# Pooling mixer's output projection with tokens on the partitions, six of its sixteen units by seven block products

## The chip, the core and the metric

The kernel runs on one core of one Trainium2 chip. The metric is the device time of one execution in microseconds (us); lower is better. A core has five engines that matter here, each with its own instruction queue, worked off strictly in order: TensorE (PE in the profile), VectorE (DVE), ScalarE (ACT), GpSimd (POOL) and SyncE (SP), which here only issues DMAs. Engines wait for one another and for DMAs through semaphores. TensorE writes its sums into PSUM, everything else lies in SBUF, 128 partitions wide.

## What is computed

A two-layer decoder trunk for 256 tokens of 2048 channels, all in float32. Layer 0 mixes tokens by causal pooling, layer 1 by dilated attention; each mixer and each convolutional feed-forward (FFN) is followed by a layer norm of the residual sum. The change touches layer 0's mixer and its norm:

```python
def pool_mixer(h, w_in, w_grp, scale, w_out):
    p = (h @ w_in).reshape(B_, S, N_POOL_GROUPS, POOL_GROUP_DIM)
    ...                                   # trailing mean over 2, 4, 8, 16 tokens, minus the token
    mixed = jnp.einsum('bsgc,gcd->bsgd', pooled, w_grp).reshape(B_, S, D) * scale
    return mixed @ w_out
...
mix = pool_mixer(h, pool_w_in[i], pool_w_grp[i], pool_scale[i], pool_w_out[i])
h = layer_norm(DEEPNORM_ALPHA * h + mix, ln1_g[i], ln1_b[i])
ff = conv_ffn(h, ...)
```

The 2048 channels are handled as four blocks of 512, and `w_out` as sixteen squares of 512 by 512.

## The kernel before

All weight products run as a list of **units** (`units`, line 69). One unit is a 512-by-512 square of a weight matrix (1 MB in float32) times 256 tokens. To keep float32 accuracy every operand is split into a high part, rounded to TensorE's fp32r format, and a low remainder; three of the four products of the parts are summed. For each weight square ScalarE casts the high part (line 99, tile `wh`) and VectorE subtracts it to get the low part (line 100, tile `wl`).

`run_units` (line 141) writes the program out by hand, and each engine works in just this order. For unit i it first calls `ahead(i)`: SyncE gets the load of unit i+5 (three raw buffers, line 41), and ScalarE and VectorE get the split of unit i+3. The pool for split weights has four buffers (line 42), so the split of unit i+3 can start only when TensorE has finished unit i-1, and must be done when unit i+2 ends. Then come TensorE's products of unit i, then callbacks that earlier units deferred with `later(n, fn)` ("n units from now", line 135), then the unit's own `post`.

Two layouts of a product occur:

- **Features on the partitions** (`mm_quad`, line 165): the weight square is the stationary operand, the tokens stream. Mode "ab" issues 16 matmuls of 512 columns (line 180) and 16 of 256 (line 181) for a unit; mode "a" issues 48 of 256 columns (lines 183 to 185). Mode "x" (also lines 183 to 185, 258 columns) serves the first unit group behind a norm, before the norm's mean and scale are known: it streams XP, the shifted residual times the norm's gain, and corrects afterwards (`norm_evac`, line 471).
- **Tokens on the partitions** (`group_tm`, line 202): the activations are stationary, the weights stream; a plain unit is 24 matmuls of 512 columns (lines 255 to 257). Here a unit can also be done by seven block products instead of eight (`mk_seven`, line 219): it stands in the list as two entries, "a" with 18 and "b" with 24 matmuls of 256 columns (lines 244 to 246). The seven products need sums of blocks of the weights: `split_sums` (line 107) has VectorE compute them (lines 120, 122, 124) beside the splits (lines 119 and 121 for "a", 113 and 114, twice each, for "b"). They also need the same sums of the activations. This form serves the FFN's down projections and the attention's V.

**Before the stage in question**, `x_quad` (line 538) transposes the loaded x (tiles `xin`) on TensorE, splits it, and copies it to the residual H, features on the partitions (line 553). Units 0 to 18 are the input projection and three of the four group products; units 19 to 35 are the sixteen output squares with the last group product as unit 21; the FFN begins at unit 36. `grp_post` (line 526) scales a group's result and splits it into the tile `mixed`.

**The stage itself** (`add_last`, line 487) has features on the partitions, twelve units in mode "ab" and the last four, which make the last column block, in mode "a". `resid_last` (line 331) adds each finished column block to H. After block 0 a matmul with ones estimates the mean of each token from these 512 channels (`shift`, line 382), and all of H is shifted by it. For blocks 1 and 2 `stats` (line 377) accumulates sums and squares, folded by VectorE and squared by ScalarE; `xp` (line 419) makes XP with four ScalarE and four VectorE instructions per block. `chain` (line 430), one unit after the last, makes mean and variance by two matmuls with ones and VectorE's reciprocal of 256 columns, and starts the normalisation.

**Transposing a finished block** exists already, between the FFN's parts: `to_tokens` and `to_features` (lines 798 and 828) transpose 32-by-32 blocks on VectorE and move the blocks to their places with sixteen DMAs of 32 KB (`moves`, line 812), all issued by SyncE in three parts of 6, 5 and 5, one, two and three units later. `early_post` (line 840) recombines the seven products; with `by_dma` GpSimd adds the result by an accumulating DMA (line 287).

Of the kernel before, what the change touches and what calls it, by code (L numbers as in the profile page):

```python
# [32 lines left out]
def trunk(ctx: ExitStack, tc: tile.TileContext, x, pool_w_in, pool_w_grp, pool_scale, pool_w_out,  # L33
# [168 lines left out]
    def group_tm(w, r0s, c0, ncol, xqs, post, apart=False, seven=(), early=None):  # L202
# [5 lines left out]
        def opened():  # L208
            t = pair("t")
            ps.append(t[:, 0, :])  # L210
            if not apart:
                ps.append(t[:, 1, :])
            if seven:
                t = pair("s")
                ps.extend([t[:, 0, :], t[:, 1, :]])
# [3 lines left out]
        def mk_seven(kind, j):  # L219
            fst, fin, op, cl = j == 0, j == len(r0s) - 1, j == opening, j == closing  # L220

            def go(h, l):
                if kind == "a" and fst:
                    opened()
                x, sums = xqs[j](), seven[j]()
# [204 lines left out]
    def chain(ps, lay, which, after):  # L430
# [9 lines left out]
        V.tensor_tensor(mr, ps[:, :T], rs, OP.mult)  # L440
        mb, rb = rm[:, 1:2, :].to_broadcast([P, 4, T]), rm[:, 0:1, :].to_broadcast([P, 4, T])
# [50 lines left out]

    PADW = 16
# [32 lines left out]
    def grp_post(g):  # L526
        def post(ps):
            mixed_q[g] = t = quad_tile("mixed")
            for m in range(4):
# [6 lines left out]
    XIN = {}  # L536

    def x_quad(q, halves=(0, 1)):
        xin = XIN
        if halves[0] == 0:  # L540
            H[q] = hp.tile([P, 4, T], F32, name="h", tag="h")
            XC[q] = quad_tile("xc")
        for half in halves:
            ps = bank("xT")
            for kk in range(2):
                for t in range(2):
                    k = 2 * half + kk
                    PE.transpose(ps[:, kk * T + t * P:kk * T + t * P + P], xin[q, t][:, k * P:(k + 1) * P], ident)
# [4 lines left out]
            before.setdefault(q, []).append(lambda s=s, pv2=pv2: A.copy(H[q][:, s, :], pv2))  # L553
# [4 lines left out]
    def add_grp(g):  # L558
# [9 lines left out]
    add_grp(1)  # L568
    mark = len(units)
    add_last(pool_w_out[0], [(512 * j, 512) for j in (3, 2, 1, 0)], [lambda j=j: mixed_q[j] for j in (3, 2, 1, 0)],  # L570
             True, 0, 0, after=lambda q: to_tokens(q))
# [222 lines left out]

    HT = {}


    def to_tokens(q):
        if q == 0:
            ST["hb"] = hp.tile([P, 4, T], F32, name="hb", tag="h")  # L800
        hb = ST["hb"]
        hf = hb.rearrange("p m t -> p (m t)")
        V.transpose(hf.rearrange("p (t m c) -> p m t c", t=2, m=4), H[q].rearrange("p m (t c) -> p m t c", t=2))

        def to():
            HT[q] = hp.tile([P, 4, T], F32, name="ht", tag="h").rearrange("p a t -> p (a t)").rearrange(
                "p (t c) -> p t c", t=2)
            return HT[q].rearrange("p t c -> p (t c)")

        moves(hf, to)  # L810

    def moves(fr, to):
        fr = fr.rearrange("p (k b j) -> p b k j", k=8, b=4)
        dst = []

        def part(i, n):
            if i == 0:
                dst.append(to().rearrange("p (k a j) -> p a k j", k=8, a=4))
            for ab in range(i, i + n):
                a, b = ab // 4, ab % 4  # L820
                nc.sync.dma_start(dst[0][32 * b:32 * b + 32, a], fr[32 * a:32 * a + 32, b])

        for k, (i, n) in enumerate(((0, 6), (6, 5), (11, 5))):
            later(k + 1, lambda i=i, n=n: part(i, n))

    def to_features(c):
        hb = hp.tile([P, 4, T], F32, name="hb", tag="h")
        hf = hb.rearrange("p m t -> p (m t)")  # L830
        V.transpose(hf.rearrange("p (m t c) -> p t m c", m=4, t=2), HT[c].rearrange("p t (m c) -> p t m c", m=4))

        def to():
            H[c] = hp.tile([P, 4, T], F32, name="h", tag="h")
            return H[c].rearrange("p m t -> p (m t)")

        moves(hf, to)


    def early_post(c, by_dma):  # L840
        def post(p16, p75):
            w = w4("w")
# [444 lines left out]
```

## Time and profile before

| | before |
|---|---|
| median of three runs | 2016.0 us (2015.46 to 2016.46) |
| profiled execution, time | 2015.77 us |
| its span in the trace | 2014.0 us |
| granted clock, mean over the core | 1.00 |
| VectorE busy | 1734.3 us |
| ScalarE busy | 1270.8 us |

How to read it: the profile is of one execution; the 1.8 us between its time and its span lie outside the instructions. Busy times on TensorE overlap, since a matmul's modelled duration runs on into the next; the spacing of the starts tells what a matmul costs. In the lists of instruction groups the columns are line, engine, operation, tiles written and read, shapes, count, then busy time in us and the mean duration in ns, then the engine's idle time before them and what ended it. In the timeline they are start in us, duration in us, engine, line, operation, tiles, shapes and count, and in brackets the idle time before and what ended it.

### The profile page before, as it was taken

The page shows a single profiled execution, that of the slowest core. Times are in us where ns is not written, and L with a number is a line of the kernel's source. Part 1 is how long each engine was busy: PE and PEld are TensorE (multiplying, and loading weights), DVE is VectorE, ACT ScalarE, POOL GpSimd, SP SyncE. Part 2 cuts the span into 40 slices and gives each one's busy share as a digit, 9 for nine tenths or more (in the row PEclk, how much of TensorE's full clock was granted, in tenths as well). Part 3 has the DMA queues.
Part 4 walks back from the last instruction along what each step waited for, and adds up shares of the span by engine and source line. Part 5 has one row for each costly group of instructions (what it writes and reads, how often), then busy time and mean ns, then how long its engine had stood idle before and what let it go on. Part 6 is the DMA issues. An engine that isn't in the chain of part 4 may idle for free.

```text
span 2014.0 us, 31469 instructions
## 1 busy us (share of the span) xinstructions
PE 2005.6 (100%) x12760; PEld 1809.8 (90%) x12760; DVE 1734.3 (86%) x1824; ACT 1270.8 (63%) x1552; POOL 93.1 (5%) x153
## 2 busy tenths in 40 slices
PE   9999999999999999999999999999999999999999
PEld 8898988999899988889888988998899989989987
DVE  6868887999899899879896878787899899989898
ACT  6444686767766676656554445487767677667673
POOL 2000000000000000000001021000000000000000
PEclk9999999999999999999999999999999999999999
DMA  8555466566656757885565657557566756666665
GB/s 264 205 205 186 163 210 192 181 221 223 198 198 200 240 179 229 227 233 188 154 220 173 208 173 204 188 188 211 167 221 202 226 184 224 206 211 190 211 211 186
DMA packets 271297, 407.77 MB, mean 202 GB/s; under 512 B 74430, under 2 KB 85588, under 8 KB 270896
## 3 DMA queue, kind: packets, MB, share of 16 engines
q1 hardware_dynamic: 259488, 388.93, 58.1%
q0 software_dynamic: 11232, 16.18, 5.4%
q8 instruction: 100, 1.64, 0.3%
q10 hardware_dynamic: 432, 0.66, 0.1%
q14 instruction: 45, 0.37, 0.1%
HBM read 380.01 MB, written 2.10 MB: 190 GB/s over the span
## 4 chain that ended last, share of the span: by engine, by line
PE 93%; DVE 4%; DMA 1%; ACT 1%; issue 0%; SPq 0%; DVEq 0%; ACTq 0%
PE acc L180 42%; PE acc L181 21%; PE s L246 3%; PE s L244 3%; PE s L245 3%; PE acc L184 2%; PE acc L185 2%; PE acc L183 2%; PE t L246 2%; PE t L244 2%; PE t L245 2%; PE t L255 1%; PE t L256 1%; PE t L257 1%; DVE wl L100 1%; ACT wh L99 1%
## 5 line engine op out<-in xcount | busy, mean ns | idle before, releaser
L180 PE MATMUL acc<-xc,wh 128*128 128x512 f32 x3264 | 1151.4, 396 | 0.0
L181 PE MATMUL acc<-xc,wl 128*128 128x256 f32 x3264 | 915.7, 281 | 0.9 <-DVE wl L100 0.9
L100 DVE TENSOR_TENSOR wl<-raw,wh 128x2048 fp32r<-128x2048 f32 (+2 forms) x304 | 654.7, 2161 | 168.9 <-ACT wh L99 167.5
L180 PEld LDWEIGHTS acc<-xc,wh 128*128 128x128 f32 x3264 | 615.9, 189 | 142.9 <-issue 0.3
L99 ACT CAST wh<-raw 128x2048 fp32r<-128x2048 f32 (+2 forms) x304 | 546.8, 1805 | 166.2 <-PE acc L180 68.3
L181 PEld LDWEIGHTS acc<-xc,wl 128*128 128x128 f32 x3264 | 615.3, 189 | 1.3 <-DVE wl L100 1.2
L113 ACT CAST wh<-raw 128x1024 fp32r<-128x1024 f32 x144 | 150.6, 1053 | 203.5 <-DVE raw L122 184.1
L114 DVE TENSOR_TENSOR wl<-raw,wh 128x1024 fp32r<-128x1024 f32 x144 | 171.8, 1221 | 11.3 <-ACT wh L113 11.3
L121 DVE TENSOR_TENSOR wl<-raw,wh 128x1536 fp32r<-128x1536 f32 x72 | 126.1, 1752 | 6.4 <-ACT wh L119 5.2
L119 ACT CAST wh<-raw 128x1536 fp32r<-128x1536 f32 x72 | 106.4, 1478 | 36.6 <-PE acc L180 28.0
L287 POOL DMA_DIRECT2D ht<-w x48 | 41.3, 1014 | 1446.4 <-DVE ht L873 721.6
L246 PE MATMUL t<-wh,g 128*128 128x256 f32 x376 | 105.7, 281 | 0.0
L244 PE MATMUL t<-wh,g 128*128 128x256 f32 x376 | 105.7, 281 | 0.0
L245 PE MATMUL t<-wl,g 128*128 128x256 f32 x376 | 105.5, 281 | 0.0
L616 ACT ACTIVATE c<-u,cv 128x256 f32<-128x256 f32 x172 | 89.6, 594 | 24.0 <-DVE f L678 17.4
L246 PE MATMUL s<-wh,xs 128*128 128x256 f32 x344 | 95.9, 279 | 0.0
L244 PE MATMUL s<-wh,xs 128*128 128x256 f32 x344 | 95.8, 279 | 0.0
L245 PE MATMUL s<-wl,xs 128*128 128x256 f32 x344 | 95.7, 278 | 0.0
L124 DVE TENSOR_TENSOR raw<-raw 128x1024 f32<-128x1024 f32 x72 | 88.2, 1225 | 2.5
L621 ACT ACTIVATE a<-u,cv 128x256 f32<-128x256 f32 x172 | 73.5, 500 | 11.9 <-DVE g L688 11.9
L607 ACT COPY u<-acc 128x512 f32<-128x512 f32 x84 | 46.9, 573 | 46.3 <-PE acc L181 46.0
L621 ACT ACTIVATE u<-u,cv 128x256 f32<-128x256 f32 x172 | 73.4, 499 | 0.0
(339 smaller groups left out, 3442.3 us busy)
## 6 DMA issues: line engine op xcount, KB each, us to landing
raw<-in_ffn_w_up_dram SPq DMA_DIRECT2D x160, 1024.0 KB, 4.9
raw<-in_ffn_w_down_dram SPq DMA_DIRECT2D x80, 1024.0 KB, 5.1
raw<-in_pool_w_out_dram SPq DMA_DIRECT2D x16, 1024.0 KB, 5.0
raw<-in_shared_w_k_dram SPq DMA_DIRECT2D x16, 1024.0 KB, 5.2
raw<-in_attn_w_q_dram SPq DMA_DIRECT2D x16, 1024.0 KB, 5.1
raw<-in_shared_w_v_dram SPq DMA_DIRECT2D x16, 1024.0 KB, 5.2
raw<-in_attn_w_o_dram SPq DMA_DIRECT2D x16, 1024.0 KB, 5.2
ht<-w POOLq DMA_DIRECT2D x50, 256.0 KB, 5.2
```

The costliest lines, as they stand in the source:

```text
L99: A.copy(wh[i][:, s], r[:, s])
L100: V.tensor_tensor(wl[i][:, s], r[:, s], wh[i][:, s].bitcast(F32), OP.subtract)
L113: A.copy(h[:, :, n], r[:, :, n])
L114: V.tensor_tensor(l[:, :, n], r[:, :, n], h[:, :, n].bitcast(F32), OP.subtract)
L119: A.copy(hs, rs)
L121: V.tensor_tensor(ls, rs, hs.bitcast(F32), OP.subtract)
L180: PE.matmul(ps[m].ap, h[:, k, c], q[:, k, :, :T], start=st, stop=False)
L181: PE.matmul(ps[m][:, :T], l[:, k, c], q[:, k, 0, :T], start=False, stop=sp)
L244: PE.matmul(to, xh, h[:, k, n], start=opens and kk == 0, stop=False)
L245: PE.matmul(to, xh, l[:, k, n], start=False, stop=False)
L246: PE.matmul(to, xl, h[:, k, n], start=False, stop=ends and kk == 1)
L621: A.activation(to[:, m, :], u[:, m, i:i + T], AF.Copy, scale=cv[:, i, j:j + 1])
```

## The change

The output projection of the pooling mixer is done with tokens on the partitions, as four column blocks of four units. The residual is x as loaded: the x tiles are now the tiles `HT` (tokens on the partitions) themselves, and the copies to H are gone. Block 0 has four plain units. Blocks 1 and 2 have the order plain, seven, plain, seven, and block 3 plain, seven, seven, plain; the six units by seven products are those whose activations come from groups 0 and 1. In the list of units the entries then are: block 0 at 19, 20, 22 and 24 (the last group product at 21, block 1's first unit at 23), block 1's rest 25 to 29, block 2 30 to 35, block 3 36 to 41, and the FFN from 42 on.

`summed` replaces `grp_post`'s work for groups 0 and 1 and makes the block sums of the activations. The statistics are VectorE's batch-norm statistics per token (`bn_stats`, one value set per partition); the shift is the mean of block 0 per token, added by ScalarE to all eight half tiles (`begin`). Each finished block goes back to features on the partitions by `to_features`, whose definition, with that of `to_tokens`, `moves` and `early_post`, stands earlier in the file; the last block's sixteen moves go at once over the queues of SyncE (seven), GpSimd (six) and ScalarE (three). XP is made six units after a block's end (two for the last block). `chain_tm` replaces `chain`: it spreads the per-token scale and mean over the partitions by four 128-column transposing matmuls, one unit after the end. The second PSUM buffer of a seven-product group is opened at its first seven-product entry.

The diff, cut to its core:

```diff
+        def opened_seven():
+            t = pair("s")
+            ps.extend([t[:, 0, :], t[:, 1, :]])
...
+    def chain_tm(mvs, lay, which, after):
+        st = w4("st")
+        for t in range(2):
+            for i, col in ((0, 3), (2, 4)):
+                A.activation(st[:, i + t, :P], onesd, AF.Copy, scale=mvs[t][:, col:col + 1])
+        def spread():
+            ps = bank("spread")
+            for i in range(4):
+                PE.matmul(ps[:, P * i:P * i + P], st[:, i, :P], ident, start=True, stop=True)
+            rm = lnp.tile([P, 4, T], F32, name="rm", tag="sq")
+            A.activation(rm[:, 0:2, :].rearrange("p a t -> p (a t)"), ps, AF.Copy, scale=float(D))
+            ...
+            normed(rm, lay, which, after)
+        later(1, spread)
...
+    def moves(fr, to, at_once=False):
...
+            for ab in range(i, i + n):
+                a, b = ab // 4, ab % 4
+                by = (nc.sync, nc.gpsimd, nc.sync, nc.gpsimd, nc.scalar)[ab % 5] if at_once else nc.sync
+                by.dma_start(dst[0][32 * b:32 * b + 32, a], fr[32 * a:32 * a + 32, b])
...
+    def summed(g, ps):
+        x = w4("mix")
+        for m in range(4):
+            A.activation(x[:, m, :], ps[m][:, :T], AF.Copy, scale=vec[0][:, 64 + 4 * g + m:65 + 4 * g + m])
+        split_act(mixed_q[g], x)
...
+        def two():
+            V.tensor_tensor(d[0], a21, a22, OP.add)
+            V.tensor_tensor(d[1], d[0], a11, OP.subtract)
+            V.tensor_tensor(d[2], a21, a11, OP.subtract)
+            V.tensor_tensor(d[3], a12, d[1], OP.subtract)
...
+            A.copy(hl[0], f)
+            V.tensor_tensor(hl[1], f, hl[0].bitcast(F32), OP.subtract)
...
+        later(1, two)
...
-            before.setdefault(q, []).append(lambda s=s, pv2=pv2: A.copy(H[q][:, s, :], pv2))
...
+    def out_post(c):
+        def post(t, ps, half=None):
+            y = HT[c][:, t, :]
+            if c == 0:
+                V.scalar_tensor_tensor(y, y, ALPHA, ps, op0=OP.mult, op1=OP.add)
+            else:
+                V.tensor_tensor(y, y, ps, OP.add)
+            if c == 3:
+                ended(t)
+            elif t == 1:
+                if c == 0:
+                    later(1, begin)
+                later(2, lambda: landed(c))
+                later(6, lambda: xp(c, 0, 0))
+        return post
+
+    def begin():
+        ST["bn"] = bn = lnp.tile([P, 2, 5, 6], F32, name="bn", tag="bn")
+        for t in range(2):
+            mv = lnp.tile([P, 6], F32, name="mv", tag="mv", bufs=2)
+            V.bn_stats(bn[:, t, 0, :], HT[0][:, t, :])
+            V.bn_aggr(mv[:, 0:2], bn[:, t, 0:1])
+            V.tensor_scalar(mv[:, 2:3], mv[:, 0:1], -1.0, None, op0=OP.mult)
+            V.tensor_scalar(bn[:, t, 0, 1::3], bn[:, t, 0, 1::3], mv[:, 0:1], None, op0=OP.subtract)
+            for c in range(4):
+                y = HT[c][:, t, :]
+                A.activation(y, y, AF.Identity, scale=1.0 if c == 0 else ALPHA, bias=mv[:, 2:3])
+
+    def landed(c):
+        if c > 0:
+            for t in range(2):
+                V.bn_stats(ST["bn"][:, t, c, :], HT[c][:, t, :])
+        to_features(c)
+
+    def ended(t):
+        ...
+        V.bn_stats(bn[:, t, 3, :], HT[3][:, t, :])
+        V.bn_aggr(mv[:, 0:2], bn[:, t, :4])
+        A.activation(mv[:, 2:3], mv[:, 1:2], AF.Sqrt, bias=epst)
+        if t == 1:
+            to_features(3, True)
+        V.reciprocal(mv[:, 3:4], mv[:, 2:3])
+        V.tensor_tensor(mv[:, 4:5], mv[:, 0:1], mv[:, 3:4], OP.mult)
+        ends.append(mv)
+        if t == 1:
+            chain_tm(ends, 0, 0, to_tokens)
+            later(2, lambda: xp(3, 0, 0))
+
-    add_last(pool_w_out[0], [(512 * j, 512) for j in (3, 2, 1, 0)], [lambda j=j: mixed_q[j] for j in (3, 2, 1, 0)],
-             True, 0, 0, after=lambda q: to_tokens(q))
+    for c, js in enumerate(((3, 2, 1, 0), (3, 1, 2, 0), (3, 1, 2, 0), (3, 1, 0, 2))):
+        sv = {i: (lambda j=j: msums[j]) for i, j in enumerate(js) if c > 0 and j < 2}
+        group_tm(pool_w_out[0], [(512 * j, 512) for j in js], 512 * c, 512, [lambda j=j: mixed_q[j] for j in js],
+                 out_post(c), seven=sv, early=early_post(c, c < 3))
...
-                XIN[q, t] = stp.tile([P, 512], F32, name=f"xin{q}{t}")
+            HT[q] = ht_tile()
```

More of the change, by code (lines that the diff above doesn't have):

```diff
@@ L224, in go @@
                     opened()
+                if kind == "a" and op:
+                    opened_seven()
                 x, sums = xqs[j](), seven[j]()
@@ L490, in add_last, with to_tokens, to, ht_tile @@
                   mode="a" if c == 3 else "ab")
+    HT = {}
+    def to_tokens(q):
+        if q == 0:
+            ST["hb"] = hp.tile([P, 4, T], F32, name="hb", tag="h")
+        hb = ST["hb"]
+        hf = hb.rearrange("p m t -> p (m t)")
+        V.transpose(hf.rearrange("p (t m c) -> p m t c", t=2, m=4), H[q].rearrange("p m (t c) -> p m t c", t=2))
+        def to():
+            HT[q] = ht_tile()
+            return HT[q].rearrange("p t c -> p (t c)")
+        moves(hf, to)
+    def ht_tile():
+        return hp.tile([P, 4, T], F32, name="ht", tag="h").rearrange("p a t -> p (a t)").rearrange(
+            "p (t c) -> p t c", t=2)
@@ new lines, in to_features, with to, early_post, post @@
+    def to_features(c, at_once=False):
+        hb = hp.tile([P, 4, T], F32, name="hb", tag="h")
+        hf = hb.rearrange("p m t -> p (m t)")
+        V.transpose(hf.rearrange("p (m t c) -> p t m c", m=4, t=2), HT[c].rearrange("p t (m c) -> p t m c", m=4))
+        def to():
+            H[c] = hp.tile([P, 4, T], F32, name="h", tag="h")
+            return H[c].rearrange("p m t -> p (m t)")
+        moves(hf, to, at_once)
+    def early_post(c, by_dma):
+        def post(p16, p75):
+            w = w4("w")
+            right, left, u5, u = (w[:, i, :] for i in range(4))
+            A.copy(left, p16[:, :256])
+            V.tensor_tensor(right, left, p16[:, 256:], OP.add)
+            V.tensor_tensor(u, right, p75[:, :256], OP.add)
+            y0, y1 = HT[c][:, 0, :], HT[c][:, 1, :]
+            w2 = w.rearrange("p a n -> p (a n)")
+            if by_dma:
+                V.tensor_tensor(w[:, 0::2, :], w[:, 0::3, :], p75[:, 256:].unsqueeze(1).to_broadcast([P, 2, 256]), OP.add)
+                ST["onto"] = [(y0, w2[:, :512]), (y1, w2[:, 512:])]
+                return
+            V.tensor_tensor(y0, y0, w2[:, :512], OP.add)
+            y1 = y1.rearrange("p (a n) -> p a n", a=2)
+            V.tensor_tensor(y1, y1, w[:, 3:4, :].to_broadcast([P, 2, 256]), OP.add)
+            yr = HT[c][:, :, :256]
+            V.tensor_tensor(yr, yr, p75[:, 256:].unsqueeze(1).to_broadcast([P, 2, 256]), OP.add)
+        return post
@@ L547, in x_quad @@
                     k = 2 * half + kk
-                    PE.transpose(ps[:, kk * T + t * P:kk * T + t * P + P], xin[q, t][:, k * P:(k + 1) * P], ident)
+                    PE.transpose(ps[:, kk * T + t * P:kk * T + t * P + P], HT[q][:, t, k * P:(k + 1) * P], ident)
             pv2 = ps.rearrange("p (k t) -> p k t", k=2)
@@ L812, in moves @@
[L812 to L824, printed above, removed]
@@ L1153, in trunk @@
         for q in range(NQ):
-            for t in range(2):
-                XIN[q, t] = stp.tile([P, 512], F32, name=f"xin{q}{t}")
+            HT[q] = ht_tile()
             halves = [slice(0, 256), slice(256, 512)] if q == 0 else [slice(0, 512)]
@@ L1185, in trunk @@
         pools["pool"] = pp
-        pools["pb"] = [pp.tile([P, 4, PADW + T], F32, name=f"pb{i}") for i in range(2)]
+        pools["pb"] = [pp.tile([P, 4, PADW + T], F32, name=f"pb{i}", tag="pb", bufs=2) for i in range(2)]
         for b in pools["pb"]:
```

73 lines of the change are left out of this document (27 added, 46 removed).

## The prediction

> **What bounds the kernel now.** I read the page first: span, engine shares, busy tenths, the chain that ended last.
>
> ```profile
> span 2014.0 us, 31469 instructions
> PE 2005.6 (100%) x12760; PEld 1809.8 (90%) x12760; DVE 1734.3 (86%) x1824; ACT 1270.8 (63%) x1552; POOL 93.1 (5%) x153
> ...
> PE 93%; DVE 4%; DMA 1%; ACT 1%; issue 0%; SPq 0%; DVEq 0%; ACTq 0%
> ```
>
> TensorE sets the time, and a shorter product shows in full as long as weights, activations and statistics keep ahead of it. VectorE, at 86%, is the next to watch. So I looked at the output projection's own stretch, 120.4 us (unit 19 starts) to 216.4 us (the FFN starts), and at its later part.
>
> ```profile
> 120.40:216.40 96.00, 96.00 (x627) 87.42 (x626) 70.82 (x74) 44.69 (x48) 0.00 (x0) 1.00 0.55 187
> 154.15:216.40 62.25, 62.25 (x419) 57.26 (x418) 50.44 (x57) 30.27 (x34) 0.00 (x0) 1.00 0.55 187
> 137.35:159.83 22.48, 22.48 (x130) 19.61 (x129) 13.88 (x13) 8.48 (x6) 0.00 (x0) 1.00 0.54 186
> ```
>
> Columns: window, its length, then busy time of PE, weight loads, DVE, ACT, POOL. VectorE works 70.8 of 96 us here, ScalarE 44.7. The third window is four "ab" units: 5.62 us each.
>
> **TensorE's part of the change.** Prices are distances between starts.
>
> ```profile
> 480.25 0.28 PE L244 MATMUL s<-wh,xs 128*128 128x256 f32 x1
> ...
> 480.84 0.28 PE L246 MATMUL s<-wh,xs 128*128 128x256 f32 x1
> 805.91 0.40 PE L255 MATMUL t<-wh,g 128*128 128x512 f32 x1
> ...
> 806.61 0.40 PE L255 MATMUL t<-wh,g 128*128 128x512 f32 x1
> 222.23 0.60 PE L431 MATMUL acc<-S,onesd 128*128 128x256 f32 x2
> 222.91 0.47 PE L183 MATMUL acc<-xp,wh 128*128 128x258 f32 x1
> 11.98 0.98 PE L548 MATMUL xT<-ident,xin 128*128 128x128 f32 x7 [0.36 <-DMA xin<-in_x_dram]
> ```
>
> Five 256-column steps take 0.59 us: 0.118 each. Three 512-column steps take 0.70: 0.233 each. A plain token-major unit is 24 x 0.233 = 5.60 us, one by seven products 42 x 0.118 = 4.96 us (entry a 2.1, b 2.8), a mode "a" unit 48 x 0.118 = 5.66. Before: 12 x 5.62 + 4 x 5.66 = 90.1 us. After: 10 x 5.60 + 6 x 4.96 = 85.8. The shift's matmul goes (0.12), and the chain's two (222.23 to 222.91: 0.68) become four of 128 columns, about 0.11 apart, seven lasting 0.98 in the row: 0.44. TensorE saves 4.3 + 0.1 + 0.2 = **4.7 us**, if nothing makes it wait.
>
> **VectorE's part.** The price of a seven-product unit's weights:
>
> ```profile
> L100 DVE TENSOR_TENSOR wl<-raw,wh 128x2048 fp32r<-128x2048 f32 x264 | 602.7, 2288 | 155.1 <-ACT wh L99 154.0
> 478.67 0.68 DVE L120 TENSOR_TENSOR raw<-raw 128x512 f32<-128x512 f32 x1
> 479.27 1.75 DVE L121 TENSOR_TENSOR wl<-raw,wh 128x1536 fp32r<-128x1536 f32 x1
> 481.06 0.69 DVE L122 TENSOR_TENSOR raw<-raw 128x512 f32<-128x512 f32 x1
> 481.78 1.22 DVE L124 TENSOR_TENSOR raw<-raw 128x1024 f32<-128x1024 f32 x1
> 482.93 2.42 DVE L114 TENSOR_TENSOR wl<-raw,wh 128x1024 fp32r<-128x1024 f32 x2
> L425 DVE SCALAR_TENSOR_TENSOR xp<-h,vec,xp 128x256 fp32r<-128x256 f32 x48 | 20.0, 479 | 0.0
> L831 DVE STREAM_TRANSPOSE hb<-ht 128x1024 f32<-128x1024 f32 x4 | 5.0, 1239 | 0.1
> L882 DVE BATCH_NORM_STATS2 bn<-ht 128x6 f32<-128x512 f32 x7 | 4.9, 694 | 0.2
> L850 DVE TENSOR_TENSOR w<-w,s 128x512 f32<-128x512 f32 x24 | 16.5, 686 | 0.8
> L845 DVE TENSOR_TENSOR w<-w,s 128x256 f32<-128x256 f32 x26 | 10.8, 414 | 9.8 <-ACT w L844 9.8
> ```
>
> Starts overlap the instruction before by some 0.08 us. A plain split costs VectorE 2.2 us; a seven-product one 4.25 + 2.3 = 6.5 us (478.67 to 485.35, less the overlap): more than TensorE's 4.96 for the unit. The split of entry i+3 may start only when TensorE has ended entry i-1, so VectorE can't work ahead of that; and a pair's two entries shorten this lead, as each counts as one.
>
> Set t = 0 at the end of block 0 (the clock of 154 us). Undisturbed, TensorE then starts its last projection unit, 41, after four plain units and six pairs: 4 x 5.60 + 6 x 4.96 = 52.2. From t = 0 VectorE has to pass, in its fixed order, before that unit's low part is ready: five pair splits (32.5; the first pair was done earlier), four plain splits (8.8), block 0's last sum and the rest of its post (1.3), `begin`'s statistics (2.4), three transposes (3.5), two recombinations of 0.4 + 0.4 + 0.7 (3.0), four sums onto HT (2.5), four statistics of 0.65 (2.5), two XP of 1.6 (3.2): **59.7 us against 52.2**. TensorE is 7.5 us late there even if VectorE waits for nobody. Behind it VectorE owes two more FFN splits (4.4) and the one after (2.2), block 3's recombination (2.7), XP of block 2 (1.6) and the last statistics (5.2), 16.1 us, while TensorE has 5.6 + 5.8 us (one plain unit, one of mode "x": 216.4 to 222.2) before the spreading matmuls stand in its queue: another 4.7 late. Floor: 7.5 + 4.7 - 4.7 = **+7.5 us**. The squares, folds and shift adds that go are already absent from this list. Ahead of t = 0 the block sums for groups 0 and 1 add about 2.2 us each to VectorE; its 26 idle us (70.8 of 96) cover them, as plain units give it 5.6 us for 2.2.
>
> **ScalarE, SyncE and the waits added.**
>
> ```profile
> L113 ACT CAST wh<-raw 128x1024 fp32r<-128x1024 f32 x144 | 150.6, 1053 | 203.5 <-DVE raw L122 184.1 <-PE t L257 6.4 <-PE acc L180 4.2
> L119 ACT CAST wh<-raw 128x1536 fp32r<-128x1536 f32 x72 | 106.4, 1478 | 36.6 <-PE acc L180 28.0 <-DMA raw<-in_ffn_w_down_dram 6.4 <-DMA raw<-in_shared_w_v_dram 1.7
> L424 ACT ACTIVATE xp<-h,vec 128x256 fp32r<-128x256 f32 x48 | 20.4, 497 | 0.0
> L920 ACT ACTIVATE ht<-ht,mv 128x512 f32<-128x512 f32 x2 | 1.3, 717 | 0.6 <-DVE mv L916 0.6
> L438 ACT ACT_TABLE_LOAD x3 | 3.8, 1283 | 0.1
> 154.35 1.91 ACT L99 CAST wh<-raw 128x2048 fp32r<-128x2048 f32 x1 [3.71 <-PE acc L180]
> L89 SPq DMA_DIRECT2D raw<-in_pool_w_out_dram x16: 367/368/371, 96.2 to 185.5; - x16
> L821 SPq DMA_DIRECT2D h<-hb x64: 585/608/1645, 771.7 to 875.3; - x64
> h<-hb SPq DMA_DIRECT2D x64, 32.0 KB, 3.7
> ht<-w POOLq DMA_DIRECT2D x50, 256.0 KB, 5.2
> ```
>
> The row at 154.35 shows the four-buffer rule: ScalarE idles until TensorE frees a weight buffer. The rows below it price a block's way back to features: SyncE needs 0.61 us to issue each of sixteen 32 KB moves, 9.7 us, with two loads of 0.37 between 10.5, and the last lands 3.7 us later: some 14 us from transpose to H. XP's ScalarE instructions wait for that landing, and behind them in ScalarE's queue stand the casts of the next weights; for those wait VectorE's subtractions and TensorE. Walked through, times from t = 0:
>
> - *Block 1's end.* `begin` puts eight ScalarE instructions (row of 717 ns, 5.2 us together) ahead of the casts of entry 29: those run 11.5 to 13.5, their subtractions 12.6 to 15.0. TensorE wants them at 12.7: 1.1 us late, and 1.6 more at unit 30, whose subtraction ends at 18.3. Sum 2.7.
> - *Block 2.* Block 0's transpose ends at 16.1, the moves are issued until 26.6 and landed at 30.3. ScalarE, free at 27.2, waits 3.1 us for XP[0]; entry 34's casts come at 32.1. Block 1's statistics, transpose and pairs follow without a pause. TensorE waits 0.9 (unit 33), 0.1, 3.4 (entry 35), 0.4: 4.8.
> - *Block 3.* Block 1's transpose ends at 39.8, landing at 53.6; ScalarE stands from 49.6. Block 2's recombination and entry 39's split come after: ready at 60.8 where TensorE came at 54.6. Waits 6.2, then 1.0 and 2.9: 10.0.
> - *The spread.* Block 2's transpose ends at 67.5, landing 81.8; ScalarE (free at 78.6) makes XP[2] until 83.6; the last sums, two square roots with a table load of 1.28 and reciprocals run on VectorE and ScalarE to 90.7; ScalarE then issues three moves (1.8) and four activations, to 93.5. TensorE came to the spread at 81.0: 12.6 us.
>
> XP[3] then comes at 103.8, wanted at 111, so it costs nothing. The accumulating DMAs (5.2 us) land before VectorE reaches the statistics that read them. At the start the residual copies (eight on ScalarE) go; waits there are for x and weights (the row at 11.98), so I count nothing either way; if the copies had delayed a cast it would be a gain under 1 us. PSUM: four buffer pairs hold here as before; zero.
>
> Sum: 2.7 + 4.8 + 10.0 + 12.6 = 30.1 us of waits, less 4.7: **+25.4 us**. On the profiled execution's 2015.77 us (0.2 below the median of 2016.0) that is 2041.2. The landing is the unknown: 2 us, nearly the shortest, gives +20, 5 us +29.
>
> **A rule about the clock.**
>
> ```profile
> 1.06 2.50 PE L1172 MATMUL warm<-one 128*128 128x128 f32 x10 [1.06 <-DVE one L1168]
> ```
>
> Ten 128-column matmuls at the start take 2.5 us, seven of the same size at 11.98 take 0.98: after a still array the first microseconds run at about half speed. The trace has no long stop later on, and the 1.00 granted in the windows says nothing of one. The Trainium skill, "TensorE: Matmul & The Clock Gate", part 1 ("What's actually happening"), says that the array falls back to half clock after an idle window of about 3.4 us; by that, and the trace's start agrees with the half speed, the stops at entry 39 and at the spread would bring it on.
>
> **The rivals.**
>
> *Faster: everything stays hidden.* 2015.8 - 4.7 = 2011. For it: TensorE is on 93% of the chain that ended last, and 144 casts of line 113 (two to a pair, 72 pairs) lie in other stages under it. Against it: 59.7 against 52.2; it decides only if VectorE passes that list in under 52 us and the landings keep nobody.
>
> *No change:* the waits just eat the 4.7, 2016. It needs VectorE's two lists (75.8 us) a tenth shorter than I count, and no landing waited for.
>
> *VectorE alone:* landings and ScalarE hidden, +7.5, 2023.3; decisive if moves are issued faster than 0.61 us or XP doesn't block.
>
> *The clock drops too:* two long stops (6.2 us at entry 39 with one matmul in it, 12.6 at the spread), each followed by some 4 us at half speed (1.06 to 5.2 at the start), about 2 us lost each: 2045.
>
> *Landings slow among the loads:* 7 us each, +35, 2051.
>
> *The change doesn't do what it says:* the seven-product entries show by their lines; I give that nothing.
>
> **How the numbers follow.** Chances: forecast 0.48, clock 0.17, VectorE alone 0.20, slow landings 0.04; no change 0.05, faster 0.06. The forecast's own range by the landing is 2036 to 2045. The range for 8 in 10 takes in VectorE alone down to 2021 and the clock with a slower landing up to 2049. A measurement here can tell about 0.2%, 4 us, from no change: slower 0.89, same 0.05, faster 0.06.
>
> **What would show it.** Right: in the stage after 154 us TensorE idles with "DVE wl" of the two lines 114 and 121 as releaser, at entries 35, 39 and 40; ScalarE idles ahead of XP with "DMA h<-hb"; the spread's matmuls wait some 12 us for the tile `st`; VectorE is near fully busy from 154 to 225; the FFN starts 8 to 12 us later than 216.4. Wrong: no idle TensorE there and a stage of 91 us (then 2011), or waits that end with VectorE alone. A granted clock below 1 after the spread would speak for the clock rival.

## The result, and the profile after it

The changed kernel takes 2051.28 us (median of 6 runs, 2049.63 to 2052.02) against 2015.86 for the kernel before in the same job (2015.46 to 2016.46): a ratio of 1.0175, 95% interval 1.0162 to 1.0188. It is slower by 35.4 us, where +25.4 was forecast and 2049 was the upper end of the range. The profiled execution took 2050.99 us, with a span of 2049.2.

The page of the changed kernel, the lines that answer to the first ones of before:

```profile
span 2049.2 us, 31450 instructions
...
PE 2012.0 (98%) x12679; PEld 1811.1 (88%) x12679; DVE 1759.0 (86%) x1856; ACT 1283.3 (63%) x1567; POOL 100.2 (5%) x163
...
PE 88%; DVE 6%; DMA 3%; ACT 2%; issue 1%; SPq 1%; ACTq 0%; DVEq 0%
```

Five points of the chain that ended last have gone from TensorE to VectorE, DMA and ScalarE. The place is found by cutting both spans where the same work starts on TensorE: unit 19, the second of the FFN's four units of mode "x" (the first behind the chain before, and behind the spreading matmuls after), and the end of that group, three units later. Windows of the kernel before, then of the changed one (columns as in the prediction):

```profile
120.40:222.91 102.51, 102.51 (x680) 93.85 (x678) 76.91 (x86) 48.85 (x55) 0.00 (x0) 1.00 0.54 185
...
222.91:240.36 17.45, 17.45 (x147) 17.42 (x145) 15.95 (x13) 13.77 (x16) 0.00 (x0) 1.00 0.45 151
```

```profile
122.75:156.40 33.65, 33.65 (x171) 28.30 (x170) 25.36 (x24) 17.68 (x19) 0.00 (x0) 1.00 0.42 141
156.40:190.30 33.90, 30.61 (x191) 26.90 (x190) 24.81 (x31) 16.44 (x19) 1.79 (x2) 1.00 0.53 147
190.30:224.60 34.30, 23.83 (x135) 20.83 (x134) 29.22 (x35) 15.90 (x21) 1.70 (x2) 0.87 0.65 177
...
256.22:275.37 19.15, 19.15 (x146) 19.15 (x146) 18.29 (x15) 16.36 (x24) 0.00 (x0) 0.89 0.70 227
```

Unit 19 starts 2.35 us later (122.75 against 120.40). From there to the second "x" unit TensorE needs 256.22 - 122.75 = 133.47 us in place of 102.51: +30.96. In what follows this stretch is called the stage. The three "x" units behind it take 1.70 more, and all of the rest of the span 0.2 more. The first block (plain units) has no idle TensorE; from 190 us on, TensorE works 23.83 of 34.30 us while VectorE works 29.22, and the granted clock is 0.87.

What TensorE waited for from 150 to 260 us (engine, waiting line, what ended the wait: total, times, longest):

```profile
PE spread L455 <- ACT st L450: 12.9, 1, 12.9
PE s L248 <- DVE wl L121: 4.8, 2, 3.4
PE s L247 <- ACT wh L119: 3.8, 2, 3.3
PE t L259 <- DVE wl L100: 3.7, 3, 1.3
PE s L248 <- DVE wl L114: 2.7, 2, 1.8
```

27.9 us, counted from the modelled end of the matmul ahead of each stop. By the distances between starts, less the 0.118 or 0.233 us that the matmul ahead takes when nothing stops it, the same ten stops cost 29.9. All of it ends with weights of the seven-product units, with the weights next to them, or with `st`. Who kept those weights? ScalarE's timeline, the instructions that stood longest:

```profile
189.71 1.71 ACT L427 ACTIVATE xp<-h,vec 128x256 fp32r<-128x256 f32 x4 [5.22 <-DMA h<-hb]
191.33 0.19 ACT L430 CAST xp<-gb 128x16 fp32r<-128x16 f32 x1
191.42 1.48 ACT L119 CAST wh<-raw 128x1536 fp32r<-128x1536 f32 x1
...
213.95 1.70 ACT L427 ACTIVATE xp<-h,vec 128x256 fp32r<-128x256 f32 x4 [5.14 <-DMA h<-hb]
215.56 0.19 ACT L430 CAST xp<-gb 128x16 fp32r<-128x16 f32 x1
215.66 0.36 ACT L572 COPY w<-s 128x256 f32<-128x256 f32 x1
215.92 1.47 ACT L119 CAST wh<-raw 128x1536 fp32r<-128x1536 f32 x1
...
244.30 1.70 ACT L427 ACTIVATE xp<-h,vec 128x256 fp32r<-128x256 f32 x4 [4.20 <-DMA h<-hb]
...
251.62 2.21 ACTq L546 DMA_DIRECT2D h<-hb  x3
253.88 1.28 ACT L450 ACTIVATE st<-onesd,mv 128x128 f32<-128x128 f32 x4 [3.06 <-issue]
```

Three times XP stands 4 to 5 us for a landing. Twice the cast of the next weights (line 119) comes behind it in the queue, the third time what the norm needs at its end. The last two rows are the three moves that ScalarE issues ahead of `st`, and `st`.

VectorE at the same place:

```profile
190.25 1.69 DVE L428 SCALAR_TENSOR_TENSOR xp<-h,vec,xp 128x256 fp32r<-128x256 f32 x4 [3.44 <-ACT xp L427]
191.85 0.69 DVE L120 TENSOR_TENSOR raw<-raw 128x512 f32<-128x512 f32 x1
192.93 1.76 DVE L121 TENSOR_TENSOR wl<-raw,wh 128x1536 fp32r<-128x1536 f32 x1 [0.39 <-ACT wh L119]
```

VectorE is idle for 3.44 us ahead of XP, and then has the weights' subtractions still to do: TensorE gets them at 194.74.

### The profile page after: what moved, and what is told of

The parts are those of the page before. It is cut to its first block, busy times and chain, and to the rows that moved or that the text cites. A ratio compares the mean times of both kernels' runs of the same rounds, so it can differ in the third digit from the quotient of the medians.

```text
span 2049.2 us, 31450 instructions
## 1 busy us (share of the span) xinstructions
PE 2012.0 (98%) x12679; PEld 1811.1 (88%) x12679; DVE 1759.0 (86%) x1856; ACT 1283.3 (63%) x1567; POOL 100.2 (5%) x163
## 4 chain that ended last, share of the span: by engine, by line
PE 88%; DVE 6%; DMA 3%; ACT 2%; issue 1%; SPq 1%; ACTq 0%; DVEq 0%
PE acc L180 39%; PE acc L181 20%; PE s L249 3%; PE s L247 3%; PE s L248 3%; PE t L249 2%; PE t L248 2%; PE t L247 2%; PE t L258 2%; PE t L259 2%; PE t L260 2%; PE acc L184 2%; PE acc L185 2%; PE acc L183 2%; DVE wl L100 2%
## 5 line engine op out<-in xcount | busy, mean ns | idle before, releaser
L100 DVE TENSOR_TENSOR wl<-raw,wh 128x2048 fp32r<-128x2048 f32 (+2 forms) x298 | 641.6, 2160 | 162.2 <-ACT wh L99 157.6
L99 ACT CAST wh<-raw 128x2048 fp32r<-128x2048 f32 (+2 forms) x298 | 535.9, 1804 | 156.7 <-PE acc L180 53.9
L113 ACT CAST wh<-raw 128x1024 fp32r<-128x1024 f32 x156 | 162.9, 1053 | 219.5 <-DVE raw L122 195.6
L114 DVE TENSOR_TENSOR wl<-raw,wh 128x1024 fp32r<-128x1024 f32 x156 | 186.1, 1222 | 16.0 <-ACT wh L113 16.0
L121 DVE TENSOR_TENSOR wl<-raw,wh 128x1536 fp32r<-128x1536 f32 x78 | 136.8, 1754 | 7.0 <-ACT wh L119 5.7
L119 ACT CAST wh<-raw 128x1536 fp32r<-128x1536 f32 x78 | 115.3, 1478 | 41.1 <-PE acc L180 24.5
L124 DVE TENSOR_TENSOR raw<-raw 128x1024 f32<-128x1024 f32 x78 | 95.6, 1225 | 2.7
```

What stands on the lines that cost most here:

```text
L99: A.copy(wh[i][:, s], r[:, s])
L100: V.tensor_tensor(wl[i][:, s], r[:, s], wh[i][:, s].bitcast(F32), OP.subtract)
L113: A.copy(h[:, :, n], r[:, :, n])
L114: V.tensor_tensor(l[:, :, n], r[:, :, n], h[:, :, n].bitcast(F32), OP.subtract)
L119: A.copy(hs, rs)
L121: V.tensor_tensor(ls, rs, hs.bitcast(F32), OP.subtract)
```

## The experiments

Four causes were held against each other: the weights of the six seven-product units are more work than VectorE has time for; ScalarE's queue stands behind XP's landings; the array's clock drops after the stops; and the start (x loaded straight into the residual's tile) runs otherwise. All times are medians, each beside the kernel before in the same job: 2015.55 us for the first four, 2015.72 for the next four, 2016.19 for the three after, 2016.30 for the last.

**Vectors held.** In the changed kernel the small vector loads on GpSimd's queue start far earlier. GpSimd's first load, in the changed kernel and then in the kernel before:

```profile
5.63 0.67 POOL L1297 DMA_DIRECT2D vrow<-in_ln_g_dram  x1 [3.78 <-ACT xc L668]
```

```profile
26.76 0.67 POOL L1194 DMA_DIRECT2D vrow<-in_ln_g_dram  x1 [24.91 <-ACT xc L551]
```

No line of the change says so: before, the vectors' tiles got the memory of the tiles of x, so their loads waited for x's last reader. (They are thirteen; the expectation below says eleven.) Two small writes hold them back again:

```
+            V.memset(r[:, 0:1], 0.0)
...
+            V.memset(cr[:, :, 0:1], 0.0)
```

> The changed kernel with one addition: a small VectorE memset on each tile of the norm's and convolution's vectors, behind the first units, so that GpSimd's eleven small loads start some 20 us later, as they did before the change. In the changed kernel they start at 5.6 us, beside the first weights and x, and the output stage starts 2.35 us later than before. Theory (these loads take the place of the first weights, and the longer stop that follows drops the array's clock): about 2.3 us faster than the changed kernel, 2049.0. Rival (x landing in the residual's own tiles, or the missing residual copies, shift the start): no change, 2051.3.

2048.16 us (2047.27 to 2050.24), 3.1 less than the changed kernel, though the two ranges just overlap; unit 19 starts at 119.2 in its profile. The early loads cost the start; a run below shows the same in the kernel before.

**The spread's stop filled.** A hundred dummy matmuls of 256 columns, whose result nobody reads, ahead of the spreading matmuls:

```
+            for i in range(100):
+                PE.matmul(ps[:, :T], ones4, XP[1][:, 0, 0, :T], start=True, stop=True)
```

> The changed kernel with 100 useless 256-column matmuls (11.8 us) ahead of the four spreading ones, which TensorE runs while it would wait 13.1 us for their operand. No other engine gets work. Theory of the clock (the stop itself makes the matmuls after it run at half speed: the three x units behind it take 19.2 us where 17.4 are due, the spread 1.9 where 0.9 are): 2.7 us faster, 2048.6. Rival (the stop is harmless, or what follows is slow for another reason): no change, 2051.3.

2047.78 us (2046.68 to 2048.91). The three "x" units behind the spread, in its windows:

```profile
253.82:271.17 17.35, 17.35 (x147) 17.35 (x146) 15.88 (x14) 15.33 (x20) 0.19 (x1) 1.00 0.71 221
```

17.35 us at a granted 1.00, against 19.15 at 0.89 in the changed kernel and 17.45 before. The "x" units' 1.70 us are the clock's, brought on by the stop at the spread. (Of the 3.5 us in the medians some is the start, which is 1.2 us earlier in this profile.)

**XP later.** XP is put further down the schedule, so that ScalarE comes to it when its data has landed:

```
-                later(6, lambda: xp(c, 0, 0))
+                later((12, 12, 7)[c], lambda: xp(c, 0, 0))
```

> The changed kernel with XP of blocks 0, 1 and 2 made 12, 12 and 7 units after the block's end instead of 6, so that ScalarE doesn't stand for the landing of the moves. Theory (VectorE has more to do than fits, and ScalarE's wait for landings adds to it): of 31 us of waits 22 stay, among them 11 at the spread: 9 to 12 us faster, about 2040. Rival (the landings alone are the cause and VectorE would keep up): nearly all waits go, about 2025.

2039.14 us (2038.73 to 2040.06): 12.1 off, so the queue behind the landings costs about a third of the loss. TensorE still waits 18.9 us, most of it now with VectorE:

```profile
PE spread L455 <- ACT st L450: 8.8, 1, 8.8
PE t L259 <- DVE wl L100: 5.5, 3, 2.4
PE s L248 <- DVE wl L114: 3.2, 2, 2.3
PE s L248 <- DVE wl L121: 1.4, 1, 1.4
```

**All units plain.** `sv` is emptied, so that none of the 16 units is done by seven products, and the entries of the schedule are moved for the shorter list:

```
-                later(2, lambda: landed(c))
-                later(6, lambda: xp(c, 0, 0))
+                later((2, 2, 1)[c], lambda: landed(c))
+                later((6, 6, 5)[c], lambda: xp(c, 0, 0))
...
-        sv = {i: (lambda j=j: msums[j]) for i, j in enumerate(js) if c > 0 and j < 2}
+        sv = {}
```

> The changed kernel with all sixteen units plain, none by seven products (block 2's landing and XP are called one unit earlier, since its block 3 has four entries instead of six; the block sums of the activations are still made). TensorE works 4.0 us longer. Theory (the seven-product splits are what VectorE can't carry): one wait of 2 to 4 us at the spread stays, plus 2.3 at the start: 2019 to 2022. Rival (the token-major form itself, with its transposes, moves and its chain at the end, is the cost): waits of over 15 us stay, above 2035.

2023.07 us (2021.64 to 2025.4), 1 us above the expected range. Only 2.4 us of waiting are left in the stage, all at the spread; a half-clock span of 6.8 us goes with that stop, and the three "x" units take 19.33 us in place of 17.45. The units by seven products, meant to save 6 x 0.64 us of TensorE, cost 28.2 us as scheduled here. Its profiled run, 2025.4, started unit 19 at 125.06, 4.66 later than before.

**All plain, with what stood in the way removed.** The vectors held, no block sums (nobody reads them now), the moves to features shared between SyncE and GpSimd, and at the end the norm's chain ahead of the last block's moves, none of them on ScalarE:

```
+            if g < 2:
+                return summed(g, ps)
...
-                by = (nc.sync, nc.gpsimd, nc.sync, nc.gpsimd, nc.scalar)[ab % 5] if at_once else nc.sync
+                by = (nc.sync, nc.gpsimd)[ab % 2] if at_once or two else nc.sync
...
-        if t == 1:
-            to_features(3, True)
...
+            to_features(3, True)
```

> Token-major with all sixteen units plain and what the other runs pointed to mended: the vectors' loads held back, no block sums of the activations, the blocks' moves issued by SyncE and GpSimd in turn, the last block's transpose and moves behind the chain's own instructions and none of them on ScalarE; landings called 2, 1, 1 and XP 6, 6, 5 units after a block's end. Theory (only VectorE's load by the seven-product splits and the queues made the change slow): waits under 2 us, TensorE 0.9 us less than before, start about 1 us earlier: 2014 to 2016.5. Rival (the token-major norm costs by itself): 2020 or more.

2017.46 us (2015.6 to 2019.36, 11 runs), ratio 1.0009 [1.0000, 1.0017]: 1.0 us above the upper end of what was expected. But the stage is as worked out. Its window:

```profile
120.92:222.48 101.56, 101.56 (x490) 84.42 (x489) 63.80 (x67) 47.53 (x51) 13.89 (x24) 1.00 0.65 192
```

No stop; 0.95 us shorter than before's 102.51, and 13 us less VectorE work. In this profile 0.5 us are lost ahead of the stage and 0.7 behind the three "x" units. Its run took 2015.99, 1.5 less than the median, so the profile does not show where the median's time goes.

**Two units by seven products,** in block 2, the rest as in that plain kernel, but with the block sums made again and the schedule moved:

```
+        sv = {i: (lambda j=j: msums[j]) for i, j in enumerate(js) if c == 2 and j < 2}
```

> As the plain mended kernel, with block 2 alone by two seven-product units (plain, seven, plain, seven), where plain units on both sides leave VectorE room; the block sums of the activations are made again; landings 2, 2, 1 and XP 8, 7, 5 units after. Theory (VectorE carries a pair or two if its lead can refill): waits of 1 to 3 us, TensorE 1.3 us less: 2013.5 to 2016. Rival (any seven-product unit here overloads VectorE): 2019 or more.

2019.33 us (2018.31 to 2020.8): 1.9 above the plain form instead of below it. The stage itself took 100.36 us, 1.2 less than plain, yet TensorE was stopped after it, in the FFN, for the tile `xc` from VectorE. A half-clock span of 3.4 us follows that stop. The instructions ahead of it:

```profile
PE acc L180 <- DVE xc L308: 2.4, 1, 2.4
...
220.79 1.25 DVE L559 STREAM_TRANSPOSE hb<-ht 128x1024 f32<-128x1024 f32 x1 [1.88 <-DMA h<-hb]
...
230.68 1.71 ACT L427 ACTIVATE xp<-h,vec 128x256 fp32r<-128x256 f32 x4 [5.20 <-DMA h<-hb]
...
237.39 2.29 DVE L100 TENSOR_TENSOR wl<-raw,wh 128x2048 fp32r<-128x2048 f32 x1 [2.08 <-ACT wh L99]
```

VectorE was not behind with its work here: it stood idle for 2.08 us until a cast of ScalarE's came, one instruction before `xc`. ScalarE had stood 5.20 us at the last block's XP (2.14 in the plain form), because that block's transpose had waited for block 2's moves. So it is a late landing again that stops TensorE. Whether the two units or the moved schedule make block 2's moves late, no run separates.

**Six units, XP later, differences left out.** This form leaves out three of VectorE's instructions (lines 120, 122 and 124) of each seven-product unit; its output is therefore not the reference's.

```
+        if state["split"] < marks[0]:
+            V.tensor_tensor(ls, rs, hs.bitcast(F32), OP.subtract)
+            return
```

> The changed kernel with XP later (12, 12, 7 units), and for the six seven-product units of this stage VectorE's three block differences of the weights (lines 120, 122, 124) left out, so the output isn't the reference's; TensorE's products, ScalarE's casts, the landings and the chain stay. Beside the kernel with XP later alone (2039.1). Theory (VectorE's load sets the waits): 2.5 us less per pair in VectorE's queue, waits fall by 6 us and a stop's clock drop goes: 2031 to 2033. Rival (the waits come from ScalarE, landings or TensorE's own order): within 2 us of 2039.

2034.74 us (2034.44 to 2036.08): 4.4 under the same kernel with them. 6 x 2.4 = 14 us less VectorE work gave back only a third of that; the wait at `st` was 8.0 us in place of 8.8, and one of 4.3 us ended with a plain split behind the pairs. So the differences are not the main part of what the six units cost in this form. This came out above the 2031 to 2033 expected. Its trace shows why the wait at `st` stayed: ScalarE's last cast in the stage stood 6.26 us for its weights, whose load SyncE issued behind six moves, VectorE idled 2.84 us for that cast, and the statistics came after it. So at its end this form is not limited by VectorE's work, and the next one spreads the moves over two queues.

**Six units, everything else mended:** as the quick plain form, but with the change's six units, and XP at 12, 12, 7.

```
+        sv = {i: (lambda j=j: msums[j]) for i, j in enumerate(js) if c > 0 and j < 2}
```

> The changed kernel with its six seven-product units kept and everything else mended: vectors' loads held, XP 12, 12, 7 units after, moves on two queues, the chain ahead of the last block's moves and off ScalarE's queue. Theory (VectorE's work alone is over TensorE's time in blocks 1 to 3): waits of some 20 us stay, 7 at the spread, and the clock drops with them: 2029 to 2034. Rival (landings, queues and the start were the cost, VectorE keeps up): 2012 to 2018.

2033.38 us (2032.03 to 2034.42), 15.9 above the plain form. With the landings and the moves out of the way it has these waits left:

```profile
PE spread L455 <- ACT st L450: 5.1, 1, 5.1
PE s L248 <- DVE wl L114: 5.0, 3, 2.3
PE t L259 <- DVE wl L100: 2.8, 3, 1.2
PE s L248 <- DVE wl L121: 0.8, 1, 0.8
```

13.7 us, where some 20 were expected. Of them 2.1 (0.9 and 1.2 us, at 169.8 and 174.2 us) come right behind `begin`, whose eight ScalarE instructions stand ahead of the casts; VectorE idles 4.75 us there. The other 11.6 come from 185 to 237.1 us, where VectorE is busy for 48.25 of 52.10 us: nearly all of that is VectorE's own work. The prediction's ledger for VectorE alone held 7.5 + 4.7 = 12.2.

**The vectors early, in the kernel before.** The start was still open, so the suspected cost was put into the old kernel by itself: its vectors' tiles get a pool of their own, opened ahead of that of x.

```
+    vctx = ExitStack()
+    vp = vctx.enter_context(tc.tile_pool(name="vecs", bufs=1))
...
-            r = pp.tile([80, P], F32, name=f"vrow{l}")
+            r = vp.tile([80, P], F32, name=f"vrow{l}")
```

> The kernel before, with one edit: the tiles of its vectors lie in a pool of their own, so that their loads no longer wait for the memory of the pool of x and start at about 5 us (they start at 26.76 us in the kernel before, at 5.63 us in the changed one). Theory (early loads of the vectors take queue and transfer time from the first weights and from x, and the longer stop drops the clock): some 2 to 3 us slower than before, 2018 to 2019. Rival (the lost time at the start comes from x in the residual's tile and from the missing copies): no change, 2015.7.

2019.03 us (2018.32 to 2021.66, 11 runs), 2.8 above the 2016.19 of the kernel before. Its unit 19 starts at 123.40, 3.00 later. TensorE's waits in its first 30 us:

```profile
PE xT L548 <- DMA xin<-in_x_dram: 2.3, 3, 1.3
PE acc L183 <- ACT wh L99: 2.0, 1, 2.0
```

In the kernel before these two are 1.0 and 1.2. With the early loads TensorE waits longer for x and for the first weights, also with x still in its old tiles. The clock, which the expectation brought in, has no part in it: this profile has no half-clock span there.

**All plain, x loaded twice.** x goes into the old tiles for the transposes, as before, and by GpSimd once more into the residual's tile, behind the vectors:

```
+        for q in range(NQ):
+            HT[q] = ht_tile()
+            for t in range(2):
+                nc.gpsimd.dma_start(HT[q][:, t, :], x[0, t * P:(t + 1) * P, 512 * q:512 * q + 512])
```

> As the quick plain form (every unit plain, 2017.46), but x is loaded as before into the tiles of the start's pool, from which it is transposed, and the vectors' loads wait for that memory as before; a second load of x by GpSimd's DMAs, behind the vectors, fills the residual's tile. Theory (the start then runs as before, and the stage is 1.0 us shorter, as in the profile of the quick plain form, 101.55 against 102.51 us): 2014.7. Rival (the missing copies or the form of the output stage itself make the start vary): 2017.5.

2017.47 us (2016.51 to 2020.21, 11 runs): the theory's 2014.7 did not come. The stage is 101.57 us, as without the second load, but in this profile (a run of 2019.97) and in the next there is a new stop, which begins at 94.0 and at 91.8 us:

```profile
PE acc L180 <- DVE pb L600: 1.3, 1, 1.3
```

The second load is issued at 40 to 49 us; VectorE's weight splits in front of that stop come 3.9 us later than in the kernel before (in the next kernel: 76.61 against 72.72).

**One unit by seven products,** the last of block 1, on top of the last kernel; block sums for group 0 alone.

```
-        sv = {}
+        sv = {i: (lambda j=j: msums[j]) for i, j in enumerate(js) if c == 1 and j == 0}
```

> As the plain form with x loaded twice, with one unit by seven products (the last of block 1), its block sums made for group 0 alone, and the schedule's landing and norm entries moved for it (landing 2, 2, 1, norm 8, 7, 5). Theory (one such unit takes about 0.8 us off TensorE and VectorE still has the slack for its sums): about 0.6 less than that plain form, 2014. Rival (any unit by seven here costs VectorE more than it has, and TensorE waits for it): 2016 or more.

2016.57 us (2015.77 to 2018.29, 11 runs), 0.9 under the plain form, with ranges that overlap. The stage shows it better:

```profile
121.38:222.35 100.97, 100.97 (x508) 84.90 (x507) 72.50 (x77) 52.19 (x57) 15.82 (x26) 1.00 0.68 198
```

0.60 less than plain, and no stop in or behind it: one such unit fits, and pays what the prediction counted for it (0.64).

**The same, the second load of x later,** meant to be spread over four units from about 79 us:

```
+        for q in range(NQ):
+            later(9 + q, lambda q=q: x_again(q))
```

> As the form with one unit by seven products and x loaded twice, but the second load of x is spread over four units from about 79 us on, where the DMA engines have a share of about 55% to carry, instead of following the vectors at 40 to 47 us. Theory (the second load took transfer time from the weights, the weights' splits came 3.9 us later, and so TensorE waited 1.3 us for the pooling's sum at about 91 us in both profiles with x loaded twice): that stop goes, the output stage starts at about 120 us, and the time is 1.0 to 1.5 us under that of the one-seven form, 2015.2, which is about 0.7 below the kernel before. Rival (the start varies from run to run for a reason that none of these edits touches): 2016.5.

2015.14 us (2013.66 to 2018.66, 11 runs), ratio 0.9994 [0.9985, 1.0003]. The median is where the theory put it, and that stop is gone. Not as it said, two of the eight loads are issued at 41.6 us and the other six together at 84.6, and the output stage started at 121.9 in this profile, whose run took 2016.36. It has the lowest median of all forms here; that it beats the kernel before is not shown, as the interval holds 1.

## Why the prediction was right in direction and wrong in size

**TensorE's saving: right.** A seven-product unit was to save 0.64 us against a plain one; one such unit shortened the stage by 0.60 (101.57 to 100.97) and two by 1.20. The plain rest was to save 4.7 - 6 x 0.64 = 0.86; measured 0.95.

**The waits: right, in place, cause and size.** By the walk, and as measured by distances between starts: block 1's end 2.7 us, 2.5 measured; block 2 4.8, 5.7; block 3 10.0, 8.6; the spread 12.6, 13.1. Together 30.1 forecast, 29.9 measured; that the sum is so near is partly luck, as blocks 2 and 3 are off by 0.9 and 1.4 us in opposite directions. The releasers, lines 114 and 121 and ScalarE behind "h<-hb", are those named, and XP's later place took 12.1 us off, as a queue that stands for a landing must give. That VectorE alone would bring 12.2 us of waits is borne out by 11.6 of the 13.7 in the form with all else mended. With that, the rivals of no change and of everything hidden are out.

Two of its signs did not come. VectorE was to be near fully busy from 154 to 225 us; it was busy for 56.25 of 71.00, in part because it too stood for ScalarE behind the landings. And the FFN was to start 8 to 12 us later than before, though the walk's own waits up to there, 2.7 + 4.8 + 10.0, less 4.3 for TensorE, already give 13.2. It started 19.0 later (235.48 against 216.45).

The rival of slow landings named 2051, just what was measured, but by chance: from a block's last move to its XP it took 4.7, 3.8 and 3.6 us, where that rival needed 7 each time and the forecast took 3.7.

**The clock: the step that failed.** The forecast's sum had nothing for it, and the rival counted two stops and about 2 us each, 4 us in all. Windows of TensorE in the changed kernel (length, busy time, granted clock, DMA share, GB/s):

```profile
195.00:199.00 4.00, 3.40 (x18) 0.57 0.23 89
219.00:226.00 7.00, 4.79 (x22) 0.52 0.44 75
246.00:256.20 10.20, 1.87 (x8) 0.53 0.28 38
256.20:261.00 4.80, 4.80 (x27) 0.57 0.85 237
```

Busy time times what was withheld: 3.40 x 0.43 + 4.79 x 0.48 + 1.87 x 0.47 = 4.6 us up to the last three "x" units (4.8 by the distances between starts), in which the clock cost another 1.7. That is three places and not two: the first lies behind stops of only 0.5 and 1.4 us with a matmul between them. In the stage, 30.96 + 4.7 - 29.9 = 5.8 us remain, of which the clock explains 4.8. Of the other 1.0 some 0.6 fall into the first microsecond behind the stops, where the first matmul lasts longer than its kind (0.38 or 0.39 us for 0.28 with 256 columns at full clock); no run here takes it apart further.

The Trainium skill, "TensorE: Matmul & The Clock Gate", part 1 ("What's actually happening"), says that the clock is set by a free-running window of about 3.4 us, and that the array is at half clock after an idle window. The trace agrees with a window that runs freely: the records of the changed kernel show the half clock in spans of 3.4, 6.8 and 13.7 us, whole multiples of 3.4. It does not agree with a need for a wholly idle window: in the 3.4 us ahead of the half clock at 195.4 only 1.9 were idle.

**The start: the other step that failed.** "I count nothing either way" was worth 2.35 us. Part of the cause is shown: the change freed the tiles of x, the vectors' loads no longer waited for their memory, and started at 5.6 us among the first weights. Held back they gave 3.1 us, and let loose in the kernel before they cost it 2.8. In the profiled run about 1.7 of the 2.35 were a half-clock span at 11.1 to 14.5 us behind the stop for the second weights. What stays open: also with the vectors held, and with x loaded as before, the start of unit 19 in the profiles lies between 119.2 and 123.7 us (1.3 of the latter is the stop at 94 us), and the times of these forms spread over 2.5 to 5 us in 11 runs. Behind the "x" units the mended forms lose another 0.6 to 0.7 us in their profiles (2.0 in the plain form with x loaded twice), for which no cause was found. In the last job the kernel before spread over 3.5 (2015.12 to 2018.63).

**The sum.** -4.7 saved, +29.9 waits, +5.8 clock and restarts in the stage, +1.7 in the "x" units, +2.35 at the start, +0.2 behind: +35.2, the difference of the two spans. Against the forecast of +25.4 the waits were 0.2 too high, and 10.0 us were not in the sum: 7.5 of clock and restarts, 2.35 of start, 0.2 behind. The chance of 0.17 for the clock was too low: a forecast whose own list has ten stops of up to 12.6 us should carry half-clock spans as a term.

## What to carry to other kernels

Saving array time by more work on the weights pays only while the engine that makes the weights has slack at that very place: here one such unit of 16 gave 0.6 us, two gave 1.2 in their stage and lost more behind it to a late landing, and six cost 28, or 16 with all else mended. Before an instruction that waits for a DMA is put into a queue, look at what stands behind it; moving one line of the schedule was worth 12 us. And where a change frees a tile, ask which later tile gets its memory: a load that used to wait may start at once, among the transfers that the beginning needs.

## What the runs showed of the hardware

Stops that empty the array for less than 2 us at a time can halve its clock for 3.4 us, and do so at no fixed distance from the stop. Three kernels have the same pair of stops on the way into one seven-product unit, with a single matmul between them. TensorE's rows behind the second stop in the changed kernel:

```profile
194.97 0.28 PE L249 MATMUL s<-wh,mixed 128*128 128x256 f32 x1
...
195.44 0.41 PE L247 MATMUL t<-wh,mixed 128*128 128x256 f32 x1
```

A 256-column matmul lasts 0.28 us in the records at full clock and 0.41 at half. In this kernel the half clock comes 0.7 us after the second stop (195.43 against 194.74). In the form with the vectors held it comes at once (191.44 against 191.36). In the one that fills the spread it does not come until after the next stop (199.20). The two stops have nearly the same lengths in all three: 0.87, 0.80 and 0.61 us, then 1.79 each time, by the distances between starts.

What differs is where a window falls. Within each trace the starts of the half-clock spans lie whole multiples of 3.413 us apart (in the changed kernel 11.11, 195.43, 219.33 and 246.63: 54, 7 and 8 times), which gives a grid of windows for each kernel. TensorE in the windows of this grid, ahead of the half clock and in it, in the changed kernel, with the vectors held and with the spread filled:

```profile
192.02:195.43 3.41, 1.53 (x8) 1.00 1.01 341
195.43:198.85 3.42, 2.97 (x15) 0.50 0.18 71
```

```profile
188.03:191.44 3.41, 1.60 (x7) 1.00 0.94 359
191.44:194.86 3.42, 3.42 (x16) 0.50 0.03 10
```

```profile
192.37:195.78 3.41, 2.14 (x18) 1.00 0.41 153
195.78:199.20 3.42, 0.39 (x4) 1.00 0.00 0
199.20:202.61 3.41, 3.41 (x17) 0.50 0.35 51
```

In the first two kernels both stops fall into one window, which leaves 1.53 and 1.60 us of work in it, and the next window is at half clock. In the third the same stops leave 2.14 us, and the clock stays until a window with 0.39. Over all fourteen traces, between 3 and 2005 us, every one of the 16 windows at full clock in which TensorE was idle for 55% or more was followed by half clock, 8 of the 14 with 47 to 55%, and none with less. So in these traces the limit is a window that is about half idle. The idle time is that between modelled matmuls, of which some can be missing, so the limit is known to a few per cent only. At the start of the program the same holds: a stop of 1.94 us for the second weights was followed by full clock in the quick plain form, one of 1.42 by half clock in the changed kernel. In a sum such spans can be counted, 1.7 us for each 3.4 that is busy throughout, but a stop near half a window can fall either way.
